# Three additions moved from GpSimd to VectorE, and parts of the retention branch issued one chunk earlier, in a two-layer decoder trunk

## The chip, the core and the metric

The kernel runs on one NeuronCore of a Trainium2 chip. A core has five instruction streams that run side by side and meet only at semaphores: TensorE (PE in the profile; its weight loads are listed as PEld), VectorE (DVE), ScalarE (ACT), GpSimd (POOL) and SyncE (SP), which here only issues weight transfers. The metric is the device time of one execution in microseconds (us), the median of several executions; lower is better.

## The reference

Two layers work on 256 tokens of width 2048 in float32. Each layer is a token mixer and a gated FFN, each behind an RMSNorm and added to the residual stream. The mixer has four branches (retention, a diagonal state-space model called S5, gated linear attention or GLA, and causal pooling). One input projection feeds them all, and it also makes one sigmoid gate per branch and channel:

```python
proj = (h @ w_in).astype(jnp.float32)
rq, rk, rv, rg, su, gq, gk, gv, gg, gr, pu, gate_logits = jnp.split(proj, _split_points(), axis=-1)
rq = rotary(rq.reshape(B_, S_, RET_HEADS, RET_DK), positions)
rk = rotary(rk.reshape(B_, S_, RET_HEADS, RET_DK), positions) * (RET_DK ** -0.5)
ra = retention(rq, rk, rv.reshape(B_, S_, RET_HEADS, RET_DV))
ya = head_norm(ra).reshape(B_, S_, BRANCH_W) * jax.nn.silu(rg)
...
branches = jnp.stack([ya, yb, yc, yd], axis=2)
up = jnp.einsum('bsnc,ncd->bsnd', branches, w_branch)
gates = jax.nn.sigmoid(gate_logits.reshape(B_, S_, N_BRANCH, D_MODEL))
merged = jnp.sum(gates * up, axis=2)
return merged @ w_out
```

Rotary is `x1*cos - x2*sin, x1*sin + x2*cos` for each head, so it ends in one addition of two products. Retention multiplies the scores of queries and keys by a causal decay and then by the values; `head_norm` normalises each of its four heads. `merged` is a sum over four branches, so three additions for each block of channels.

## The kernel before

**The weight stream.** All large products run through chunks. A chunk is 128 x 1024 weights (512 KB): SP brings it into one of three `raw` buffers, ScalarE casts it to `hi` (L262), VectorE subtracts to get `lo <- raw, hi` (L263), and TensorE multiplies first by `hi` and then by `lo`. `hi` and `lo` have three buffers each. In the mixer most chunks go through `mm_xs` (matmuls at L362, eight with `hi` and four with `lo`), where the activations `X` are the weights and the streamed side is `hi` or `lo`. Every chunk thus needs one cast of ScalarE and one subtraction of VectorE in time.

**The side work.** Branches are written as Python generators. After the instructions of each chunk have been emitted, `pump()` lets every started generator that is due go on to its next `yield`; `yield n` means that the next part comes n chunks later. TensorE's instructions stay in the order in which they are written, so the numbers behind `yield` set the place of each branch's matmuls between the chunks. The other engines are ordered by a scheduler with priorities: what stands under `with prio():` is put ahead of side work, as far as its inputs allow; the rest comes later.

**The places that matter here.** `retention` turns queries and keys (tile `rqk`, and `rot`, a copy with halves swapped) by two products on VectorE (L492, L493) and one addition on GpSimd (L494); then come the scores of two pairs of heads (L505), their product with the decay (tiles `P1`, `P2`, L508 and L509), the product with the values (L514 to L516), and `head_out`. `head_out` normalises on VectorE into `hy`, transposes `hy` on TensorE in two pairs of heads (L470) and splits each transposed pair into `br[:, :, 0]` and `br[:, :, 1]` (ScalarE's cast at L262 and VectorE's subtraction at L263, tile `br`). GLA uses the same `head_out`. Its first matmuls are L525 (tiles `grT`, `wg`) and L549 (tile `gqk`). All of these take their PSUM from `psmall()`, two buffers in turn, so a matmul of the side work waits until the buffer two requests back has been read. `up` adds a branch into the merged sum `mg` (L878): on GpSimd, except for the very last block. S5 uses GpSimd for four additions and subtractions in each of its steps (L747, L748, L758, L759), between products on VectorE.

Of the kernel before, what the change touches and what calls it, by code (L numbers as in the profile page):

```python
# [15 lines left out]
ALU = mybir.AluOpType  # L16
# [136 lines left out]
def trunk(ctx: ExitStack, tc, d, outT, dbg=None):  # L153
# [54 lines left out]
    def C(name):  # L208
        o, w = CON[name]
        return con[:, o:o + w]  # L210
# [10 lines left out]
    tt = nc.vector.tensor_tensor  # L221
# [3 lines left out]
    ptt = nc.gpsimd.tensor_tensor  # L225
# [4 lines left out]
    def order(then):  # L230

        tc.add_manual_dep(then.ins, anchor[0].ins.name, NOSYNC, reason="order")
        return then

    def prio(offset=4000):
        return tc.high_priority(offset=offset)
# [21 lines left out]
    def psmall():  # L258
        return P.small()

    def split(hi, lo, src):
        i = nc.scalar.copy(hi, src)  # L262
        tt(lo, src, hi.bitcast(F32), op=ALU.subtract)  # L263
        return i
# [82 lines left out]
    def mm_xs(kt, rows, X):  # L347

        ps = P.main.tile([128, 2, 512], F32, tag="mp", name="mp")
        for c in range(0, kt, 2):  # L350
            hi, lo, n = load(2, rows(c * 128, (c + 2) * 128))
            xs_chunk(ps, kt, c, hi, lo, X, (0, 1))
            pump()
        return ps
# [80 lines left out]
    def bc(ap, n):  # L435

        return ap.unsqueeze(1).to_broadcast([128, n, T])
# [4 lines left out]
    def head_out(pool, ops, sg, r, br, wait):  # L442

        st = pool.tile([128, 8, 6], F32, tag="hst", name="hst", bufs=1)
        mv = pool.tile([128, 8, 2], F32, tag="hmv", name="hmv", bufs=1)
        for t in range(2):
            for i in range(4):
                nc.vector.bn_stats(st[:, 4 * t + i, :], ops[t][:, i * 128:(i + 1) * 128])
        for i in range(8):
            nc.vector.bn_aggr(mv[:, i, :], st[:, i, :])  # L450
        ve = pool.tile([128, 8], F32, tag="hve", name="hve", bufs=1)
        ts(ve, mv[:, :, 1], EPS, None, op0=ALU.add)
        rs = pool.tile([128, 8], F32, tag="hrs", name="hrs", bufs=1)
        ptt(rs, ve, C("mhalf")[:, 0:8], op=ALU.pow)
        y = pool.tile([128, 2, 512], F32, tag="k4", name="hy", bufs=6)
        for t in range(2):
            ts(rs[:, 4 * t:4 * t + 4], rs[:, 4 * t:4 * t + 4], r[:, t:t + 1], 0.5,
               op0=ALU.mult, op1=ALU.mult)
            for i in range(4):
                ts(y[:, t, i * 128:(i + 1) * 128], ops[t][:, i * 128:(i + 1) * 128],  # L460
                   mv[:, 4 * t + i, 0:1], rs[:, 4 * t + i:4 * t + i + 1],
                   op0=ALU.subtract, op1=ALU.mult)
        tt(y, y, sg, op=ALU.mult)
        yield wait
        for i in range(4):
            if i % 2 == 0:
                ps = psmall()
            for t in range(2):
                o = (i % 2) * T + t * 128
                nc.tensor.transpose(ps[:, o:o + 128], y[:, t, i * 128:(i + 1) * 128], ident)  # L470
            if i % 2 == 1:
                s = ps[:, :].rearrange("p (a t) -> p a t", a=2)
                split(br[:, i - 1:i + 1, 0], br[:, i - 1:i + 1, 1], s)
                yield 2

    def silu_gate(pool, ps, rh):

        sg = pool.tile([128, 2, 512], F32, tag="k4", name="sg", bufs=6)
        with prio():
            for t in range(2):  # L480
                act(sg[:, t], ps[:, t], AF.Tanh, scale=rh[:, t:t + 1])
                stt(sg[:, t], sg[:, t], 1.0, ps[:, t], op0=ALU.add, op1=ALU.mult)
        return sg

    def retention(pool, qk, rv, sg, r, br):
        rot = pool.tile([128, 4, T], F32, tag="k4", name="rot", bufs=6)

        for b in (0, 32, 64, 96):
            o = b ^ 32
            order(nc.scalar.dma_start(rot[b:b + 32], qk[o:o + 32]))  # L490
        yield 3
        tt(rot, rot, bc(sinr, 4), op=ALU.mult)  # L492
        tt(qk, qk, bc(cosr, 4), op=ALU.mult)  # L493
        ptt(rot, rot, qk, op=ALU.add)  # L494
        yield 8
        dec = pool.tile([128, 4, T], F32, tag="k4", name="dec", bufs=6)
        order(nc.scalar.dma_start(dec, d["decay"].rearrange("p (h t) -> p h t", h=4)))
        P1 = pool.tile([128, 4, T], F32, tag="k4", name="P1", bufs=6)
        P2 = pool.tile([128, 4, 128], F32, tag="k2", name="P2", bufs=4)
        for a in range(2):  # L500
            pss = [psmall(), psmall()]
            for o, sc, t0 in ((0, slice(0, 128), 0), (T, slice(128, T), 128)):
                for j, ps in enumerate(pss):
                    b = slice(64 * j, 64 * j + 64)
                    nc.tensor.matmul(ps[:, o:o + T - t0], rot[b, 2 + a, sc], rot[b, a, t0:T],  # L505
                                     start=(o == 0), stop=True, **MM)
            for j, ps in enumerate(pss):
                tt(P1[:, 2 * a + j], ps[:, 0:T], dec[:, 2 * a + j, :], op=ALU.mult)  # L508
                tt(P2[:, 2 * a + j], ps[:, T:384], dec[:, 2 * a + j, 0:128], op=ALU.mult)  # L509
            yield 2  # L510
        ops = [psmall(), psmall()]
        for hd in range(4):
            e = slice(hd * 128, (hd + 1) * 128)
            nc.tensor.matmul(ops[0][:, e], P1[:, hd, 0:128], rv[:, 0, e], start=True, stop=True, **MM)  # L514
            nc.tensor.matmul(ops[1][:, e], P1[:, hd, 128:T], rv[:, 0, e], start=True, stop=False, **MM)
            nc.tensor.matmul(ops[1][:, e], P2[:, hd], rv[:, 1, e], start=False, stop=True, **MM)  # L516
        yield from head_out(pool, ops, sg, r, br, 12)

    def gla(pool, l, V, qk, grT, gv, sg, r, br):
        wg = pool.tile([32, 256], F32, tag="k1", name="wg", bufs=1)  # L520
# [80 lines left out]
        for hd in range(4):  # L601
# [6 lines left out]
            nc.tensor.matmul(ops[1][:, e], A[:, j, a0 + 128:a0 + 256], gv[:, 1, e],  # L608
                             start=False, stop=True, **MM)
        yield from head_out(pool, ops, sg, r, br, 8)  # L610

    def pooling(pool, l, V, ps, rb, br):
# [204 lines left out]
    def wcols(w, c0, n):  # L817
        return lambda r0, r1: [w[r0:r1, c0:c0 + n]]
# [22 lines left out]
    def mixer(l, V, X, R, outer, pool):  # L841
# [20 lines left out]
        def gate(n, blk):  # L862

            ps = projx(C_GATE + n * D + blk * 512)
            th = outer.tile([128, 2, 512], F32, tag="th", name="th", bufs=1)
            with prio():
                for t in range(2):
                    act(th[:, t], ps[:, t], AF.Tanh, scale=rh[:, t:t + 1])
            return th

        def up(n, blk, br, th, m, first=False):
            ps = mm_xs(4, wcols(d["w_branch"][l, n], blk * 512, 512), br)
            with prio():
                if first:
                    stt(m, th, 1.0, ps, op0=ALU.add, op1=ALU.mult)
                else:
                    stt(th, th, 1.0, ps, op0=ALU.add, op1=ALU.mult)  # L877
                    (tt if n == 1 and blk == 3 else ptt)(m, m, th, op=ALU.add)  # L878


        ps = proj(C_PU)
        r, rb = R.r, R.rb
# [26 lines left out]
        sg = silu_gate(pool, ps, rh)  # L909
        br_ret = branch_tiles(outer)  # L910
        start(retention(pool, rqk, rv, sg, r, br_ret))

        gqk = pool.tile([128, 4, T], F32, tag="k4", name="gqk", bufs=6)
# [12 lines left out]
        sg = silu_gate(pool, ps, rh)  # L926
# [13 lines left out]
        for n, br in ((3, br_pool), (0, br_ret), (2, br_gla)):  # L940
            for blk in range(4):
                th = gate(n, blk)
                up(n, blk, br, th, mg[:, :, blk * 512:(blk + 1) * 512], first=(n == 3))
# [7 lines left out]
        split_scaled(br_s5[:, :, 0], br_s5[:, :, 1], y5, 0.25)  # L951
        ths = [gate(1, 0)]
        return mg, gate, up, br_s5, ths

    def turn(mg, blk, M):
# [13 lines left out]
    for l in range(DEPTH):  # L969
        last = l + 1 == DEPTH  # L970
        with tc.tile_pool(name=f"mix{l}", bufs=1, reuse_waits="tile") as outer, ExitStack() as mixb:
            with narrow(l):
                with tc.tile_pool(name=f"mixa{l}", bufs=1, reuse_waits="tile") as pool:
                    mg, gate, up, br_s5, ths = mixer(l, V, X, R, outer, pool)
                pool = mixb.enter_context(tc.tile_pool(name=f"mixb{l}", bufs=1, reuse_waits="tile"))
# [36 lines left out]
        with tc.tile_pool(name=f"ffn{l}", bufs=1, reuse_waits="tile") as pool, extra_raw(l):  # L1012
            G = pool.tile([128, KF, 2, T], F32R, tag="g", name="G")
            wup = d["w_up"][l]
            for b0 in range(0, KF, 2):
# [6 lines left out]
                with prio():  # L1022
                    u = pool.tile([128, 4, T], F32, tag="u", name="u")
                    uc = pool.tile([128, 4, T], F32, tag="uc", name="uc")
                    n = 2 * nt
                    for i, ps in enumerate(pss):
                        m = slice(2 * i, 2 * i + 2)
# [18 lines left out]
            for k, n in ((0, 4), (4, 4), (8, 4), (12, 3), (15, 1)) if last else ((0, 4), (4, 4), (8, 4), (12, 4)):  # L1046
                m = slice(k, k + n)
# [37 lines left out]
```

## Time and profile before

| what | value |
|---|---|
| time, median of 3 runs | 2987.28 us (2987.2 to 2988.97) |
| the profiled execution's own time | 2986.73 us |
| its span, first to last instruction | 2984.9 us |
| TensorE busy | 2950.4 us (99%) |
| VectorE busy | 2104.4 us (71%) |
| ScalarE busy | 1524.7 us (51%) |
| GpSimd busy | 381.8 us (13%) |
| mean granted TensorE clock | 0.996 of full speed |

The first mixer runs from the start to about 690 us, its FFN to about 1480 us; the second layer repeats this to the end. In a row of a timeline the first number is the start and the second the duration; `xN` counts merged instructions, and square brackets hold the idle time of the engine just before the row and who ended it. TensorE's matmuls overlap in the profile (each is shown longer than its turn), so progress is read from start to start.

### The profile page before, as it was taken

The page shows a single profiled execution, that of the slowest core. Times are in us where ns is not written, and L with a number is a line of the kernel's source. Part 1 is how long each engine was busy: PE and PEld are TensorE (multiplying, and loading weights), DVE is VectorE, ACT ScalarE, POOL GpSimd, SP SyncE. Part 2 cuts the span into 40 slices and gives each one's busy share as a digit, 9 for nine tenths or more (in the row PEclk, how much of TensorE's full clock was granted, in tenths as well). Part 3 has the DMA queues.
Part 4 walks back from the last instruction along what each step waited for, and adds up shares of the span by engine and source line. Part 5 has one row for each costly group of instructions (what it writes and reads, how often), then busy time and mean ns, then how long its engine had stood idle before and what let it go on. Part 6 is the DMA issues. An engine that isn't in the chain of part 4 may idle for free.

```text
span 2984.9 us, 42650 instructions
## 1 busy us (share of the span) xinstructions
PE 2950.4 (99%) x15952; PEld 2525.5 (85%) x15952; DVE 2104.4 (71%) x2712; ACT 1524.7 (51%) x1906; POOL 381.8 (13%) x371
## 2 busy tenths in 40 slices
PE   8999999999999999999999999999999999999998
PEld 8877887888888888888898788878888888888887
DVE  7798888556677777755568888885567777776445
ACT  5545545444555555544444555554445555555443
POOL 6311122010000000000053111221010000000001
PEclk9999999999999999999999999999999999999999
DMA  7765666666566666666576566666666666666554
GB/s 228 200 181 163 188 178 186 206 189 212 187 188 191 191 187 195 193 196 195 181 209 196 164 179 179 185 186 205 188 212 186 193 186 192 190 187 193 187 180 148
DMA packets 416176, 565.87 MB, mean 190 GB/s; under 512 B 24736, under 2 KB 258656, under 8 KB 415968
## 3 DMA queue, kind: packets, MB, share of 16 engines
q1 hardware_dynamic: 404960, 545.58, 59.7%
q10 hardware_dynamic: 11008, 17.57, 1.9%
q8 instruction: 125, 2.05, 0.3%
q14 instruction: 83, 0.68, 0.1%
HBM read 554.66 MB, written 4.19 MB: 187 GB/s over the span
## 4 chain that ended last, share of the span: by engine, by line
PE 91%; DVE 4%; issue 1%; DMA 1%; ACT 1%; POOL 0%; SPq 0%; DVEq 0%; ACTq 0%; POOLq 0%
PE mp L339 38%; PE mp L362 30%; PE mp L342 20%; DVE lo L263 2%; PE mp L320 2%; DMA raw<-w_in 1%; PE ps L578 1%; ACT hi L262 1%; DVE s L757 0%; PE pbu L767 0%; PE ps L961 0%; DVE s_cos L737 0%; PE pbu L796 0%; DMA h<-xT 0%; DMA raw<-w_branch 0%
## 5 line engine op out<-in xcount | busy, mean ns | idle before, releaser
L263 DVE TENSOR_TENSOR lo<-raw,hi 128x1024 fp32r<-128x1024 f32 (+2 forms) x1043 | 1319.0, 1267 | 752.9 <-ACT hi L262 748.6
L262 ACT CAST hi<-raw 128x1024 fp32r<-128x1024 f32 (+2 forms) x1043 | 1084.9, 1041 | 1199.9 <-PE mp L339 682.9
L339 PE MATMUL mp<-X,hi 128*128 128x512 f32 x3136 | 1088.7, 394 | 0.0
L342 PE MATMUL mp<-X,lo 128*128 128x256 f32 x3136 | 869.8, 277 | 0.6 <-DVE lo L263 0.6
L339 PEld LDWEIGHTS mp<-X,hi 128*128 128x128 f32 x3136 | 588.0, 187 | 135.8
L362 PE MATMUL mp<-hi,X 128*128 128x512 f32 x2560 | 641.9, 393 | 0.0
L342 PEld LDWEIGHTS mp<-X,lo 128*128 128x128 f32 x3136 | 589.3, 188 | 1.0 <-DVE lo L263 0.9
L362 PEld LDWEIGHTS mp<-hi,X 128*128 128x128 f32 x2560 | 478.1, 189 | 103.2 <-issue 1.4
L339 PE MATMUL mp<-G,hi 128*128 128x512 f32 x1376 | 477.2, 390 | 0.0
L342 PE MATMUL mp<-G,lo 128*128 128x256 f32 x1376 | 388.1, 282 | 0.0
L362 PE MATMUL mp<-lo,X 128*128 128x512 f32 x1280 | 344.5, 391 | 5.0 <-DVE lo L263 5.0
L339 PEld LDWEIGHTS mp<-G,hi 128*128 128x128 f32 x1376 | 258.3, 188 | 54.1
L362 PEld LDWEIGHTS mp<-lo,X 128*128 128x128 f32 x1280 | 240.3, 188 | 59.1 <-DVE lo L263 9.3
L342 PEld LDWEIGHTS mp<-G,lo 128*128 128x128 f32 x1376 | 260.2, 189 | 0.1
L381 POOL TENSOR_TENSOR ss<-ss,sq 128x256 f32<-128x256 f32 x55 | 56.9, 1034 | 1464.2 <-ACT sq L380 1454.9
L339 PE MATMUL mp<-M,hi 128*128 128x512 f32 x512 | 177.9, 391 | 0.0
L342 PE MATMUL mp<-M,lo 128*128 128x256 f32 x512 | 144.4, 282 | 0.0
L362 PE MATMUL mp<-hi,br 128*128 128x512 f32 x512 | 130.2, 396 | 0.2 <-ACT hi L262 0.2
L362 PEld LDWEIGHTS mp<-hi,br 128*128 128x128 f32 x512 | 95.5, 188 | 23.8 <-issue 0.8
L878 POOL TENSOR_TENSOR mg<-mg,th 128x1024 f32<-128x1024 f32 x22 | 69.7, 3170 | 352.2 <-DVE th L877 342.9
L339 PEld LDWEIGHTS mp<-M,hi 128*128 128x128 f32 x512 | 96.1, 188 | 20.1
L1033 ACT ACTIVATE uc<-u,vec 128x256 f32<-128x256 f32 x172 | 89.6, 591 | 15.0 <-DVE u L1030 15.0
(228 smaller groups left out, 2134.0 us busy)
## 6 DMA issues: line engine op xcount, KB each, us to landing
raw<-w_in SPq DMA_DIRECT2D x383, 512.0 KB, 3.8
raw<-w_up SPq DMA_DIRECT2D x688, 256.0 KB, 3.3
raw<-w_down SPq DMA_DIRECT2D x152, 512.0 KB, 4.3
raw<-w_branch SPq DMA_DIRECT2D x64, 512.0 KB, 4.3
raw<-w_out SPq DMA_DIRECT2D x64, 512.0 KB, 4.4
raw<-w_down SPq DMA_DIRECT2D x21, 384.0 KB, 3.8
rB<-sB ACTq DMA_DIRECT2D x8, 384.0 KB, 4.9
U<-us ACTq DMA_DIRECT2D x96, 32.0 KB, 3.4
```

Source lines behind the costliest of these rows:

```text
L262: i = nc.scalar.copy(hi, src)
L263: tt(lo, src, hi.bitcast(F32), op=ALU.subtract)
L320: nc.tensor.matmul(ps[:, j, :], a[:, k, sl], X[:, kk, b, :], start=(kk == 0 and i == 0 and j % 2 == 0), stop=(kk == kt - 1 and i == 2), **MM)
L339: nc.tensor.matmul(ps.rearrange("p a t -> p (a t)"), hi[:, k, sl], X[:, kk].rearrange("p a t -> p (a t)"), start=(kk == 0), stop=(kk == kt ...
L342: nc.tensor.matmul(ps[:, 0], lo[:, k, sl], X[:, kk, 0, :], start=False, stop=(kk == kt - 1), **MM)
L362: nc.tensor.matmul(ps[:, j, :], X[:, c + k, a, j * 128:(j + 1) * 128], w[:, k, :], start=(c + k == 0 and a == 0 and w is hi), stop=(c + k ...
L381: (tt if k >= 12 else ptt)(ss, ss, sq, op=ALU.add)
L578: nc.tensor.matmul(ps[:, i * 128:(i + 1) * 128], x, x, start=True, stop=True, **MM)
L878: (tt if n == 1 and blk == 3 else ptt)(m, m, th, op=ALU.add)
L1033: act(uc[:, j], u[:, j], AF.Identity, bias=V("cb", ci), scale=V("cw2", ci))
```

## The change

Four edits. The addition that ends the rotation (L494 before, L495 after) and the additions of the merged sum (L878 before, L879 after) are issued on VectorE; all of the latter were on GpSimd but the last block's. Scores, and with them what follows in the retention generator, come one chunk earlier (`yield 8` to 7), and the transposes of `hy` one more (wait 12 to 11). In `head_out` the second pair of heads follows the first after one chunk, not two (`yield 2` to 1), for GLA too, and the split of a transposed pair gets priority. One line is added, so line numbers behind L472 are higher by one after the change.

```diff
@@ head_out
             if i % 2 == 1:
                 s = ps[:, :].rearrange("p (a t) -> p a t", a=2)
-                split(br[:, i - 1:i + 1, 0], br[:, i - 1:i + 1, 1], s)
-                yield 2
+                with prio():
+                    split(br[:, i - 1:i + 1, 0], br[:, i - 1:i + 1, 1], s)
+                yield 1
@@ retention
         tt(rot, rot, bc(sinr, 4), op=ALU.mult)
         tt(qk, qk, bc(cosr, 4), op=ALU.mult)
-        ptt(rot, rot, qk, op=ALU.add)
-        yield 8
+        tt(rot, rot, qk, op=ALU.add)
+        yield 7
...
-        yield from head_out(pool, ops, sg, r, br, 12)
+        yield from head_out(pool, ops, sg, r, br, 11)
@@ up
                     stt(th, th, 1.0, ps, op0=ALU.add, op1=ALU.mult)
-                    (tt if n == 1 and blk == 3 else ptt)(m, m, th, op=ALU.add)
+                    tt(m, m, th, op=ALU.add)
```

TensorE, from GLA's matmul L525 to its matmul L549, in the order of before (`grT`, `wg`: GLA's gate; `con`, `hy`: the transposes of the retention output; `gqk`: GLA's queries and keys):

```order
L525 MATMUL ps<-grT,wg 128x256 x2
L362 MATMUL mp<-hi,X 128x512 x8
L362 MATMUL mp<-lo,X 128x512 x4
L362 MATMUL mp<-hi,X 128x512 x8
L362 MATMUL mp<-lo,X 128x512 x4
L470 MATMUL ps<-con,hy 128x128 x4
L362 MATMUL mp<-hi,X 128x512 x8
L362 MATMUL mp<-lo,X 128x512 x4
L362 MATMUL mp<-hi,X 128x512 x8
L362 MATMUL mp<-lo,X 128x512 x4
L470 MATMUL ps<-con,hy 128x128 x4
L549 MATMUL ps<-gqk 128x128 x8
```

The same stretch of TensorE's order after the change, where L525 is L526 and L549 is L550:

```order
L470 MATMUL ps<-con,hy 128x128 x4
L526 MATMUL ps<-grT,wg 128x256 x2
L362 MATMUL mp<-hi,X 128x512 x8
L362 MATMUL mp<-lo,X 128x512 x4
L470 MATMUL ps<-con,hy 128x128 x4
L362 MATMUL mp<-hi,X 128x512 x8
L362 MATMUL mp<-lo,X 128x512 x4
L362 MATMUL mp<-hi,X 128x512 x8
L362 MATMUL mp<-lo,X 128x512 x4
L362 MATMUL mp<-hi,X 128x512 x8
L362 MATMUL mp<-lo,X 128x512 x4
L550 MATMUL ps<-gqk 128x128 x8
```

Before, the second transposes stood directly in front of L549. After, three chunks lie between them, and one chunk and L526 lie between the first and the second transposes.

VectorE around the rotation, in the order of before:

```order
L493 TENSOR_TENSOR rqk<-rqk,cosr 128x1024
L263 TENSOR_TENSOR gr_1530<-wgr,gr_1530 128x16x16
L263 TENSOR_TENSOR lo<-raw,hi 128x1024
L853 TENSOR_TENSOR gqk<-gqk,mp 128x512
L263 TENSOR_TENSOR lo<-raw,hi 128x1024
L860 TENSOR_TENSOR gqk<-gqk,rb 128x512
```

The same place of VectorE after the change:

```order
L494 TENSOR_TENSOR rqk<-rqk,cosr 128x1024
L263 TENSOR_TENSOR gr_1530<-wgr,gr_1530 128x16x16
L263 TENSOR_TENSOR lo<-raw,hi 128x1024
L854 TENSOR_TENSOR gqk<-gqk,mp 128x512
L495 TENSOR_TENSOR rot<-rot,rqk 128x1024
L861 TENSOR_TENSOR gqk<-gqk,rb 128x512
L263 TENSOR_TENSOR lo<-raw,hi 128x1024
```

The addition L495 and the scaling L861 now stand ahead of the second `lo`. The additions of the merged sum stand in VectorE's order behind one `lo` that follows the gating product L878.

## Rows read from the trace of the kernel before

**Rows 1.** The page, busy time, share of the span, instructions:
```profile
PE 2950.4 (99%) x15952; PEld 2525.5 (85%) x15952; DVE 2104.4 (71%) x2712; ACT 1524.7 (51%) x1906; POOL 381.8 (13%) x371
```
**Rows 2.** TensorE's waits: us in total, times, longest us:
```profile
PE ps L549 <- DVE br L263: 6.1, 2, 3.9
PE mp L362 <- DVE lo L263: 5.0, 10, 1.3
```
**Rows 3.** Timeline, TensorE at L549, first layer, then second layer:
```profile
220.80 1.98 PE L362 MATMUL mp<-hi,X 128*128 128x512 f32 x8
222.62 1.07 PE L362 MATMUL mp<-lo,X 128*128 128x512 f32 x4
...
226.76 1.16 PE L549 MATMUL ps<-gqk 64*128 64x128 f32 x14 [2.22 <-DVE br L263]
227.85 3.28 PE L362 MATMUL mp<-hi,X 128*128 128x512 f32 x8
230.92 1.53 PE L362 MATMUL mp<-lo,X 128*128 128x512 f32 x4
...
1704.03 2.07 PE L549 MATMUL ps<-gqk 64*128 64x128 f32 x14 [3.93 <-DVE br L263]
1706.03 3.78 PE L362 MATMUL mp<-hi,X 128*128 128x512 f32 x8
```
**Rows 4.** Windows: busy PE, PEld, DVE, ACT, POOL; granted clock; DMA:
```profile
1700.00:1710.00 10.00, 6.07 (x25) 4.93 (x25) 7.46 (x17) 5.34 (x11) 0.00 (x0) 0.66 0.35 105
```
**Rows 5.** Timeline, the split behind the second transposes, second layer:
```profile
1702.14 0.56 ACT L262 CAST br<-ps 128x512 fp32r<-128x512 f32 x1
...
1703.30 0.68 DVE L263 TENSOR_TENSOR br<-ps,br 128x512 fp32r<-128x512 f32 x1
```
**Rows 6.** Timeline around the rotation's addition, first layer:
```profile
155.09 2.57 POOL L494 TENSOR_TENSOR rot<-rot,rqk 128x1024 f32<-128x1024 f32 x1
...
155.34 3.41 DVE L263 TENSOR_TENSOR lo<-raw,hi 128x1024 fp32r<-128x1024 f32 x1
...
158.80 1.20 PE L362 MATMUL mp<-lo,X 128*128 128x512 f32 x4 [1.33 <-DVE lo L263]
...
159.27 1.21 DVE L263 TENSOR_TENSOR lo<-raw,hi 128x1024 fp32r<-128x1024 f32 x1
```
**Rows 7.** Timeline around a merged-sum addition, first layer, near 490 us:
```profile
485.94 3.24 POOL L878 TENSOR_TENSOR mg<-mg,th 128x1024 f32<-128x1024 f32 x1 [0.36 <-DVE th L877]
...
486.86 2.48 DVE L737 TENSOR_SCALAR s_cos<-s_cos 128x256 f32<-128x256 f32 x1
...
491.12 1.21 PE L362 MATMUL mp<-lo,X 128*128 128x512 f32 x4 [0.70 <-DVE lo L263]
...
498.24 0.97 PE L362 MATMUL mp<-lo,X 128*128 128x512 f32 x3 [0.55 <-DVE lo L263]
```
**Rows 8.** Timeline, another merged-sum addition, near 362 us:
```profile
359.41 0.28 DVE L737 TENSOR_SCALAR s_cos<-s_cos 128x256 f32<-128x256 f32 x1
...
362.24 3.26 POOL L878 TENSOR_TENSOR mg<-mg,th 128x1024 f32<-128x1024 f32 x1 [4.69 <-issue]
...
363.82 2.76 DVE L263 TENSOR_TENSOR lo<-raw,hi 128x1024 fp32r<-128x1024 f32 x1
```
**Rows 9.** Windows, columns as in rows 4, the end of the side work:
```profile
400.00:500.00 100.00, 98.29 (x463) 79.39 (x462) 90.50 (x147) 48.97 (x59) 25.57 (x23) 1.00 0.59 177
```
**Rows 10.** The merged sum's tile: the last block's addition on VectorE, ns:
```profile
L878 DVE TENSOR_TENSOR mg<-mg,th x2: 1218/1218/1219, 686.8 to 2164.8; 128x1024 f32<-128x1024 f32 x2
```
**Rows 11.** Timeline, L525, first transposes and their split, first layer:
```profile
210.98 1.12 PE L525 MATMUL ps<-grT,wg 32*128 32x256 f32 x4
...
217.62 0.60 PE L470 MATMUL ps<-con,hy 128*128 128x128 f32 x4
...
220.16 0.57 ACT L262 CAST br<-ps 128x512 fp32r<-128x512 f32 x1
...
220.89 0.68 DVE L263 TENSOR_TENSOR br<-ps,br 128x512 fp32r<-128x512 f32 x1
```

## The prediction

> **What bounds the kernel now.** I read the page first: TensorE is busy 2950.4 us of a span of 2984.9 us [rows 1], so no engine's busy time can be shortened to good effect unless TensorE waits for it, and no edit takes a matmul away. The question is what TensorE waits for, and the list of its waits answers it. Apart from the start and the end of the program two kinds are left: L549 waits twice for the subtraction that fills `br`, 6.1 us together, and matmuls with `lo` wait ten times for VectorE's L263, 5.0 us together [rows 2]. Then I read the timeline at each of them. At L549 the wait is 2.22 us in the first layer and 3.93 us in the second [rows 3]; the reader is to see there that the matmuls behind it are slow as well, and in the table of windows that the granted clock is 0.66 between 1700 and 1710 us [rows 4]: behind an idle TensorE the clock stands at the lower of its two levels, 1.2 instead of 2.4 GHz, for a while. The `lo` waits lie where VectorE has most to do: one at the rotation [rows 6], three in a row near 490 us, the first and the last of which are shown [rows 7], and their counterparts in the second layer. From 400 to 500 us VectorE is busy 90.50 of 100 us [rows 9].
>
> **The wait at L549 (term 1).** It is there because the second transposes stand directly in front of L549 and L549 needs their buffer back, which is free only when both halves of the split are done. In the second layer the cast starts at 1702.14 and the subtraction ends at 1703.98 [rows 5], late because other casts and subtractions were put ahead. Its cost:
> - first layer: 2.22 idle; then eight `hi` matmuls in 3.28 instead of 1.98, and four `lo` ones in 1.53 instead of 1.07 [rows 3]: 2.22 + 1.30 + 0.46 = 3.98 us;
> - second layer: 3.93 idle; then L549's fourteen in 2.07 instead of 1.16, and eight `hi` matmuls in 3.78 instead of 1.98 [rows 3]: 3.93 + 0.91 + 1.80 = 6.64 us.
>
> Together 10.6 us. After the change three chunks stand between the second transposes and this matmul. A chunk takes TensorE 2.73 us (twelve matmuls; 222.62 - 220.80 for eight) [rows 3], so the split has 8.2 us, against the 3.95 us that the first split took (below). I count the whole 10.6 us as gone; what keeps L549 waiting next would be the conversion of L525's result, which is issued a chunk earlier than the second split.
>
> **What is late next (term 2, a loss).** The second transposes now need the buffer of the first ones, with only L525 and one chunk between: 0.35 + 1.06 + 2.73 = 4.1 us from the first transposes to the second (L525 takes about its 1.12) [rows 3, 11]. Before, the first split ended 221.57 - 217.62 = 3.95 us after the first transposes [rows 11]. With the same delays the wait would be nothing. The priority brings ScalarE's cast forward, but VectorE's half still stands behind two `lo` subtractions (1.21 each), the copy into `grT` and a few S5 products; counting these from the moment `grT` can be written, VectorE ends it about 1 us late. Bounds: 0, and a wait as long as 3.93 with the slow matmuls behind it. I take 1.0 us for each layer, without the slow clock, since the 1.33 us wait of rows 6 is followed by `lo` matmuls of 1.20 in all, near the usual 1.07: a loss of 2.0 us. Behind the waiting transposes stand the chunks of the stream; they resume at once, because `hi` and `lo` get filled meanwhile.
>
> **Rotation's addition on VectorE and scores a chunk earlier (term 3).** The addition takes GpSimd 2.57 us, and the `lo` subtraction issued beside it takes 3.41 instead of 1.21 [rows 6]: VectorE stood still for 2.2 us, and TensorE 1.33. On VectorE an addition of this shape takes 1.22 (the last block's is one already) [rows 10], so VectorE has 1.0 us more here, and the `lo` that was late is 2.2 us earlier. But TensorE then reaches the scores sooner, and the scores stand a chunk earlier too. They need the addition. On VectorE it ends near 158.4 us: 155.34 + 1.21 for the `lo`, some 0.6 for an addition of half the size, and 1.22. Without its wait TensorE is there at the same time: 158.80 - 1.33 + 0.91 for four matmuls [rows 3, 6]. The products with the decay, the products with values and GLA's L525 follow, each with less time in front than before. So I let half of the 1.33 come back, 0.6 us. In the second layer this wait is small already, and I count nothing. Ends: the whole 1.33 gained; or 1.5 us lost in each layer, a wait of the same length at a score or at the values.
>
> **Merged-sum additions on VectorE (term 4).** Eleven a layer leave GpSimd. On GpSimd one takes 3.24 us, and the VectorE instruction beside it is held: L737 takes 2.48 instead of 0.28, a `lo` 2.76 instead of 1.21 [rows 6 to 8], so 2.20 and 1.55 us are lost on VectorE against 1.22 for the addition itself [rows 10]. That is a gain of 1.0 us at 486 us and of 0.3 at 362. Five of a layer's eleven lie before the last of the three waits; the others come when the side work is over, where no wait for `lo` is in the list, and are worth nothing either way. TensorE waits 0.70 first and 0.55 last of three near 490 us, some 1.7 us a layer. VectorE is what is late there, so each us that it saves comes off: 1.0 us a layer, 2.0 in all. Ends: 1.7 a layer; or a loss of 5 x 1.22 = 6.1 a layer if holding is not saved (the second rival).
>
> A rule of the Trainium skill stands against these two terms: Perfetto Trace Analysis, "Optimizing Scalar/DVE Operations", says that work may well be given to GpSimd where VectorE is saturated, and adds that the two share an SBUF read port, so it may not help. SBUF — State Buffer, "Who interferes with whom", sharpens the second half: whichever starts first holds the port for its whole instruction. The held rows agree with the second half; by the first alone the sum would end on the slow side, as in the second rival.
>
> **The rest.** GLA's second transposes come a chunk earlier as well; nothing waits behind them in the list of waits, and I count 0 (ends: 0.5 either way). The load of the decay table moves on ScalarE's queue with the scores, ahead of one cast: one issue, and I count 0 (end: a cast later by less than one `lo`, 1.2 us, in each layer). SP's order of weight loads is unchanged.
>
> **Sum.** -10.6 + 2.0 - 0.6 - 2.0 = -11.2 us. Against the profiled execution's own 2986.73 us that gives 2975.5; the median of the runs is 0.55 higher, so I forecast 2976 us.
>
> **The rivals.**
> - *All of it comes back.* Neither the second transposes nor the scores wait, and the ten `lo` waits go: -10.6 - 5.0 = -15.6, so 2971.5 us. For it: priority on the split, and 8.2 us of room. Against: VectorE is 90% busy and gets 1.22 us for every addition. 17 in 100.
> - *VectorE becomes the bound, slower than before.* Its place is 360 to 500 us of each mixer. If the held time of rows 7 and 8 is only time that VectorE would have waited anyhow for ScalarE's cast or for a transfer, nothing is saved: six additions a layer (five and the rotation's) cost 1.22 each on the path, 14.6 us in all, against the 10.6 of term 1: +4.0, so 2991 us. It decides once less than about 0.9 us of each hold is saved (12 additions, 10.6 us). For it: three waits for `lo` in a row near 490. Against: L737 needs only data that ScalarE had long made, and its 2.48 us end with GpSimd's addition. 4 in 100.
> - *The wait only moves.* The second transposes wait as long as L549 did, with the slow clock behind; terms 3 and 4 alone remain: -2.6, so 2984.5 us. For it: two buffers in turn, one chunk of room, and a 3.95 us split against 4.1. Against: the cast has priority now. 10 in 100. That the edits do not do what they say can be left out: the order shows them.
>
> **How the numbers follow.** My forecast has the other 69 in 100; its own range is 2973 to 2980, from term 2 between 0 and 4 and term 3 at its ends. The range of 8 in 10 reaches into the first rival and most of the way to the third: 2970 to 2983. A measurement of this kernel tells 0.2%, 6 us, from no change: below 2981.3 is faster. Forecast and first rival lie there but for about 2 in 100: 84. Within: 12, the third rival and those 2. Slower: 4.
>
> **What would show it.** In the profile after, TensorE's wait at L550 (once L549) for `br` is gone, and the clock stays at 1.00 there. A wait of about 1 us stands at the second transposes. The `lo` beside the rotation takes 1.2 us, L738 0.3 us, and the three waits near 490 us are below 1 us together. I am wrong if TensorE's granted clock falls in the same place, if L470 waits more than 2 us, or if waits for `lo` add up to more than 5 us.

## The result and the profile after

The changed kernel takes 2966.93 us, median of 4 runs (2965.81 to 2969.09), against 2987.24 us (2986.61 to 2988.97) for the kernel before: a ratio of 0.9935, 95% interval 0.9923 to 0.9947, or 20.3 us less. The forecast was 2976, its range 2970 to 2983. The direction was right; the gain came out nearly twice as large, and 3 us beyond the low end. The profiled execution took 2965.81 us, span 2964.0, mean granted clock 0.998.

Busy time first. The row answers to [rows 1]:

```profile
PE 2938.8 (99%) x15952; PEld 2521.9 (85%) x15952; DVE 2091.4 (71%) x2736; ACT 1525.8 (51%) x1906; POOL 324.7 (11%) x347
```

VectorE has 24 instructions more, each of 1.22 us, and is nevertheless busy 13 us less: it is held less often, and that saves more than it took over. Then TensorE's waits, the whole list, to be set against [rows 2]:

```profile
PE mp L320 <- ACT hi L262: 6.4, 2, 5.7
PE mp L320 <- DVE lo L263: 2.4, 3, 1.1
PE ps L395 <- DVE ss L381: 2.0, 1, 2.0
PE ps L607 <- DVE gA L599: 1.6, 2, 0.9
PE ps L408 <- DVE dg L404: 1.5, 1, 1.5
PE mp L342 <- DVE lo L263: 0.3, 1, 0.3
```

L550 (L549 before) and all ten `lo` waits at L362 are gone; L607 is new. The other five belong to the start, the norms, the FFN and the end, where nothing was changed.

**The place of term 1.** TensorE at L550 in the first layer, against [rows 3]; then the windows around it in both layers, against [rows 4], with the same columns:

```profile
219.81 1.16 PE L550 MATMUL ps<-gqk 64*128 64x128 f32 x16
220.91 2.11 PE L362 MATMUL mp<-hi,X 128*128 128x512 f32 x8
```
```profile
219.00:229.00 10.00, 10.00 (x55) 8.03 (x55) 8.88 (x18) 8.33 (x14) 0.00 (x0) 1.00 0.54 154
1690.00:1700.00 10.00, 10.00 (x46) 8.23 (x46) 9.29 (x19) 7.17 (x12) 0.73 (x2) 1.00 0.58 164
```

All sixteen matmuls run in one piece, the `hi` ones behind them take their usual 2.1 us, and the granted clock is 1.00, the 2.4 GHz level, where it was 0.66 on the mean.

**The place of term 2.** TensorE from the first to the second transposes, then the VectorE instructions that matter in this stretch, against [rows 11]:

```profile
206.66 0.60 PE L470 MATMUL ps<-con,hy 128*128 128x128 f32 x4
207.18 1.13 PE L526 MATMUL ps<-grT,wg 32*128 32x256 f32 x4
208.24 2.12 PE L362 MATMUL mp<-hi,X 128*128 128x512 f32 x8
210.19 1.07 PE L362 MATMUL mp<-lo,X 128*128 128x512 f32 x4
211.10 0.60 PE L470 MATMUL ps<-con,hy 128*128 128x128 f32 x4
```
```profile
204.90 0.40 DVE L935 TENSOR_TENSOR grT<-ps,rb 32x256 f32<-32x256 f32 x1
...
209.44 0.68 DVE L263 TENSOR_TENSOR br<-ps,br 128x512 fp32r<-128x512 f32 x1
```

No bracket stands at the second transposes: they come 4.44 us behind the first ones, and the split is done after 3.46 (209.44 + 0.68 - 206.66).

**The place of term 3.** VectorE at the rotation, against [rows 6], then TensorE with both pairs of scores:

```profile
153.53 1.21 DVE L263 TENSOR_TENSOR lo<-raw,hi 128x1024 fp32r<-128x1024 f32 x1
...
155.27 1.21 DVE L495 TENSOR_TENSOR rot<-rot,rqk 128x1024 f32<-128x1024 f32 x1
```
```profile
156.81 0.92 PE L506 MATMUL ps<-rot 64*128 64x256 f32 x8
...
163.35 0.92 PE L506 MATMUL ps<-rot 64*128 64x256 f32 x8
```

The `lo` beside the addition takes 1.21 us, not 3.41, and the addition ends at 156.48, 0.3 us ahead of the scores. Before, the second scores looked like this, in the weight loads and then in the matmuls:

```profile
169.35 0.29 PEld L505 LDWEIGHTS ps<-rot 64*128 64x128 f32 x2 [0.52 <-DVE P L509]
169.35 1.45 PE L505 MATMUL ps<-rot 64*128 64x256 f32 x8
169.88 0.73 PEld L505 LDWEIGHTS ps<-rot 64*128 64x128 f32 x6 [0.23 <-DVE P L509]
```

Eight matmuls of the same shape were drawn over 1.45 us instead of 0.92, because they waited for the decay products before and inside the group. The list of TensorE's waits [rows 2] does not show this wait, and I had not seen it.

**The place of term 4.** VectorE near 478 us, against [rows 7], where L737 took 2.48:

```profile
477.51 1.21 DVE L879 TENSOR_TENSOR mg<-mg,th 128x1024 f32<-128x1024 f32 x1
478.65 1.21 DVE L263 TENSOR_TENSOR lo<-raw,hi 128x1024 fp32r<-128x1024 f32 x1
479.79 0.28 DVE L738 TENSOR_SCALAR s_cos<-s_cos 128x256 f32<-128x256 f32 x1
```

The window of [rows 9], where VectorE was busy 90.50 of 100 us:

```profile
400.00:500.00 100.00, 99.12 (x470) 81.15 (x469) 84.33 (x141) 53.28 (x63) 18.82 (x17) 1.00 0.62 186
```

The three waits near 490 are gone. Before, the held L737 of [rows 7] and one product more stood ahead of the next `lo`:

```profile
489.38 0.42 DVE L743 TENSOR_TENSOR s<-pbu,s_cos 128x256 f32<-128x256 f32 x1
489.83 1.23 DVE L263 TENSOR_TENSOR lo<-raw,hi 128x1024 fp32r<-128x1024 f32 x1
```

Now this `lo` stands directly behind the addition, and L738 and the product after it come later. Ahead of it VectorE spends 1.21 us instead of 2.48 + 0.42: 1.0 of that is the forecast saving (2.20 held, less 1.22), the other 0.7 is the new order, which the forecast did not have.

**The new wait** stands at GLA's product with the values. VectorE first, then TensorE:

```profile
414.47 1.22 DVE L879 TENSOR_TENSOR mg<-mg,th 128x1024 f32<-128x1024 f32 x1
415.61 0.42 DVE L599 COPY gA<-ps 128x256 f32<-128x256 f32 x1
415.94 1.22 DVE L263 TENSOR_TENSOR lo<-raw,hi 128x1024 fp32r<-128x1024 f32 x1
417.08 0.42 DVE L599 COPY gA<-ps 128x256 f32<-128x256 f32 x1
```
```profile
417.64 0.46 PE L607 MATMUL ps<-gv,gA 128*128 128x128 f32 x2 [0.88 <-DVE gA L599]
```

The merged sum's addition now stands in VectorE's own order ahead of the copies into `gA`, so the second copy, behind one more `lo`, is late.

**Where the 20.9 us of the two profiled executions lie.** TensorE has 15,136 matmuls into `mp`, in the same order in every kernel here. Taking the start of the n-th in one trace from that of the n-th in the trace before gives the time gained or lost up to there, and the difference of two such numbers that of a stage. Both layers together, in us (minus is gained); stages between those named are within 0.2 us, and the two FFNs within 0.02 (0.11 with the `head_out` edit alone). The column of the rotation ends ahead of L525, so it also holds a small `lo` wait at 200.71 us and one at 1676.26 us (0.17 and 0.19 listed):

| kernel | start | rotation to second scores | L525 to L549 and behind | GLA's values | near 490 and 1970 | all |
|---|---|---|---|---|---|---|
| the changed kernel | -1.5 | -4.5 | -11.4 | +1.9 | -5.45 | -21.0 |
| merged sum alone on VectorE | -0.6 | -0.1 | +0.1 | +2.1 | -5.45 | -4.0 |
| rotation alone on VectorE | -1.0 | -3.1 | -0.1 | -0.3 | -0.3 | -4.8 |
| `head_out` edit alone | +0.2 | -0.2 | -8.1 | +0.5 | +1.5 | -6.0 |
| scores and transposes moved alone | -0.3 | -0.2 | -11.4 | -0.3 | -0.1 | -12.3 |
| changed, both additions back on GpSimd | -0.3 | -0.2 | -11.4 | +0.2 | +1.6 | -10.1 |
| changed, without the `head_out` edit | -1.3 | -4.4 | -11.4 | +2.3 | -5.45 | -20.3 |
| changed, without priority for the split | -0.1 | -4.1 | -11.4 | +2.4 | -5.45 | -18.6 |
| changed, idle GpSimd additions added | -0.5 | -4.5 | -11.4 | +10.4 | -5.2 | -11.2 |
| changed, priority for the copies into `gA` | -0.4 | -4.2 | -11.4 | -0.3 | -5.45 | -21.7 |
| the same without the `head_out` edit | +0.2 | -4.5 | -11.4 | -0.3 | -5.45 | -21.4 |

The start, 150 us in which no kernel differs from another, varies from +0.2 to -1.5 between executions. The 1.5 that the changed kernel's profile shows there is chance, not a gain. The cost of a slow clock varies too: with the rotation alone the place of L549 is 1.3 us slower in the first layer and 1.4 faster in the second, at waits of nearly the same length (2.06 and 3.67 us), and the -0.1 in the table is their sum.

### The profile page after: what moved, and what is told of

It reads as the page before. It is cut to its first block, busy times and chain, and to the rows that moved or that the text cites. A ratio compares the mean times of both kernels' runs of the same rounds, so it can differ in the third digit from the quotient of the medians.

```text
span 2964.0 us, 42589 instructions
## 1 busy us (share of the span) xinstructions
PE 2938.8 (99%) x15952; PEld 2521.9 (85%) x15952; DVE 2091.4 (71%) x2736; ACT 1525.8 (51%) x1906; POOL 324.7 (11%) x347
## 4 chain that ended last, share of the span: by engine, by line
PE 98%; DVE 1%; ACT 0%; DMA 0%; issue 0%; POOL 0%; SPq 0%; DVEq 0%; ACTq 0%; POOLq 0%
PE mp L339 39%; PE mp L362 35%; PE mp L342 20%; PE mp L320 2%; PE ps L579 1%; DVE lo L263 0%; PE pbu L768 0%; PE pbu L797 0%; PE ps L962 0%; ACT hi L262 0%; DMA h<-xT 0%; DVE hg L1065 0%; DVE X L268 0%; PE ps L470 0%; PE ps L932 0%
## 5 line engine op out<-in xcount | busy, mean ns | idle before, releaser
L263 DVE TENSOR_TENSOR lo<-raw,hi 128x1024 fp32r<-128x1024 f32 (+2 forms) x1043 | 1286.7, 1235 | 743.5 <-ACT hi L262 740.3
L362 PE MATMUL mp<-hi,X 128*128 128x512 f32 x2560 | 639.1, 392 | 0.0
L362 PEld LDWEIGHTS mp<-hi,X 128*128 128x128 f32 x2560 | 476.5, 188 | 101.9 <-issue 1.2
L362 PE MATMUL mp<-lo,X 128*128 128x512 f32 x1280 | 342.7, 390 | 0.0
L362 PEld LDWEIGHTS mp<-lo,X 128*128 128x128 f32 x1280 | 240.4, 188 | 50.0
L362 PE MATMUL mp<-hi,br 128*128 128x512 f32 x512 | 130.2, 396 | 0.0
L362 PEld LDWEIGHTS mp<-hi,br 128*128 128x128 f32 x512 | 95.7, 188 | 23.2 <-issue 0.8
L342 PEld LDWEIGHTS mp<-M,lo 128*128 128x128 f32 x512 | 97.0, 190 | 0.1
```

The source lines that it names most:

```text
L342: nc.tensor.matmul(ps[:, 0], lo[:, k, sl], X[:, kk, 0, :], start=False, stop=(kk == kt - 1), **MM)
L362: nc.tensor.matmul(ps[:, j, :], X[:, c + k, a, j * 128:(j + 1) * 128], w[:, k, :], start=(c + k == 0 and a == 0 and w is hi), stop=(c + k ...
```

## The experiments

My theory was that each term stands for itself: moves end the wait at L549, VectorE's additions end the held instructions, nothing else matters. The rivals were that `head_out`'s edit (priority, one chunk instead of two) is what makes the gain; that the additions gain nothing by themselves; and that the gain of VectorE's additions has nothing to do with holding.

**Merged sum alone.** The kernel before with

```diff
-                    (tt if n == 1 and blk == 3 else ptt)(m, m, th, op=ALU.add)
+                    tt(m, m, th, op=ALU.add)
```

> The kernel before with one edit: all additions of the merged sum on VectorE. Theory A (a GpSimd addition holds the VectorE instruction beside it; 1.2 us on VectorE are cheaper than 1.5 to 2.2 us held): the three waits for lo near 490 us and near 1970 us go, TensorE gains 2.7 to 3.2 us at each, and GLA's product with the values (L605 to L608) waits 0.9 to 1.3 us in each layer because an addition now stands ahead of the copies L598; the wait at L549 stays. About -3.6 us, so 2983.6. Rival B (the waits near 490 went because the side work before them had moved up): the waits near 490 stay at 0.4 us or more each, and the time is 2987 or above.

Measured: 2982.68 against 2985.9, ratio 0.9987 (0.9978 to 0.9997), 3.2 us less. Its waits:

```profile
PE ps L549 <- DVE br L263: 6.0, 2, 3.9
...
PE ps L606 <- DVE gA L598: 1.9, 2, 1.1
PE mp L362 <- DVE lo L263: 1.8, 4, 1.2
```

The `lo` waits fall from ten to four; those left are at the rotation and at 201 us, and their counterparts in the second layer; the wait for `gA` comes with this edit and with no other.

**Rotation alone.** The kernel before with

```diff
-        ptt(rot, rot, qk, op=ALU.add)
+        tt(rot, rot, qk, op=ALU.add)
```

> The kernel before with one edit: the rotation's addition on VectorE. Theory A: the lo beside it takes 1.2 us instead of 3.4, its wait (1.33 us idle, 1.5 from start to start, in the first layer; 0.4 in the second) goes, and as the scores stay where they were nothing new waits: -1.9 to -2.5 us, so 2985. Rival B (that wait went because the scores were moved): it stays, and the time is within 1 us of before.

Measured: 2983.8 against 2985.9, ratio 0.9992 (0.9983 to 1.0002): by the times alone it can't be told from no change. The trace decides where the times can't. The wait of 1.33 us at the rotation is gone, the `lo` there takes 1.21, and the stage is 3.1 us shorter, both layers together. L549 stays:

```profile
PE ps L549 <- DVE br L263: 5.7, 2, 3.7
PE mp L362 <- DVE lo L263: 3.3, 6, 0.9
```

**`head_out` alone.** The kernel before with

```diff
-                split(br[:, i - 1:i + 1, 0], br[:, i - 1:i + 1, 1], s)
-                yield 2
+                with prio():
+                    split(br[:, i - 1:i + 1, 0], br[:, i - 1:i + 1, 1], s)
+                yield 1
```

> The kernel before with the edit of head_out alone: priority for the split, and one chunk instead of two between the transposes. One chunk (2.73 us) then stands between the second transposes and GLA's L549 (now L550). Theory A (the wait there is the latency of the split, and the slow matmuls behind follow a long wait): the split with priority ends some 3 to 3.5 us after the transposes, so 0.3 to 1 us of wait is left and no slow clock: -9.5 to -11 us, so about 2977. Rival C (priority is not what shortens the split; VectorE's queue is): 2 us of wait are left in each layer and the clock falls again in one of them, -4 to -6 us.

Measured: 2980.61 against 2985.9, ratio 0.9983 (0.9973 to 0.9992). The place gives 8.1 us, less than expected, since the wait is shortened and not ended. The matmul in both layers, then the window of the second:

```profile
225.24 1.16 PE L550 MATMUL ps<-gqk 64*128 64x128 f32 x14 [0.67 <-DVE br L263]
...
1699.34 1.16 PE L550 MATMUL ps<-gqk 64*128 64x128 f32 x14 [1.54 <-DVE br L263]
```
```profile
1698.00:1706.00 8.00, 6.66 (x38) 5.58 (x39) 7.30 (x15) 6.36 (x11) 0.00 (x0) 1.00 0.46 132
```

What goes first is the clock's share: behind a wait of 1.54 us the granted clock stays at 1.00 and the fourteen matmuls take 1.16 us, where behind 3.93 us they took 2.07 [rows 3]. The total, 5.3 us less, lies in the range that was given for rival C, but not for its reason: the waits are shorter than 2 us and the clock does not fall. What was not expected is a loss behind L550, 0.5 us at GLA's values and 1.5 near 490 and 1970 (table). It appears again below, where `head_out`'s edit stands with the additions on GpSimd, and not where they are on VectorE; no run shows its cause.

**The moves alone.** The kernel before with

```diff
-        yield 8
+        yield 7
...
-        yield from head_out(pool, ops, sg, r, br, 12)
+        yield from head_out(pool, ops, sg, r, br, 11)
```

> The kernel before with the two moved yields alone (scores one chunk earlier, transposes one more); no priority, and two chunks between the transposes as before. Two chunks (5.5 us) then stand between the second transposes and L549. Theory A (chunks in front of L549 are what counts): split without priority takes 4 to 4.9 us, the wait is gone, and so is the slow clock: -11 to -12 us at this place. At the scores TensorE still waits for the addition on GpSimd, now a chunk nearer: 1 to 2 us more there in the first layer. In all -9 to -11, so about 2977. Rival C (priority is what counts): a wait of 1 us or more stays at L549.

Measured: 2975.96 against 2985.9, ratio 0.9965 (0.9952 to 0.9978). Two numbers changed by one make about half of the gain: L549 is gone from the list without `head_out`'s edit, since two more chunks now stand between the second transposes and it. Most waits for `lo` stay, and the second scores, a chunk earlier, now show theirs in the list:

```profile
PE mp L362 <- DVE lo L263: 4.7, 8, 1.2
...
PE ps L505 <- DVE P L509: 1.0, 2, 0.5
```

That costs 0.4 us in each layer, less than the 1 to 2 expected, and the small `lo` waits at 201 and 1676 us, which are gone here, give back 0.5 each.

**The changed kernel without `head_out`'s edit.** That edit undone, the rest kept.

```diff
-                with prio():
-                    split(br[:, i - 1:i + 1, 0], br[:, i - 1:i + 1, 1], s)
-                yield 1
+                split(br[:, i - 1:i + 1, 0], br[:, i - 1:i + 1, 1], s)
+                yield 2
```

> The changed kernel with the edit of head_out undone (no priority, two chunks between the transposes): three of the four edits. Theory A (with the moved yields alone, two chunks stood in front of L549 and its wait was gone, 12.3 us at the end of the two stages): L549 does not wait here either, and the time is within 1.5 us of the changed kernel's, about 2967. Rival C (VectorE, which now has the additions too, needs the priority): a wait of 0.5 us or more at L549 or at the second transposes, 2 us or more in all.

Measured: 2966.9 against 2987.02, ratio 0.9932 (0.9917 to 0.9946): the changed kernel's time. The rival that this edit makes the gain falls.

**Without the priority alone.** The split is issued as before, `yield 1` stays.

```diff
-                with prio():
-                    split(br[:, i - 1:i + 1, 0], br[:, i - 1:i + 1, 1], s)
+                split(br[:, i - 1:i + 1, 0], br[:, i - 1:i + 1, 1], s)
```

> The changed kernel without the priority of the split, its one chunk between the transposes kept. Forecast's term (the second transposes wait for the first split, 4.1 us of room against 4 us): a wait of 0.5 to 1.5 us at L470 in each layer, 1 to 3 us in all. Rival: the split has time anyway; no wait at L470, within 0.5 us of the changed kernel in the profile.

Measured: 2966.94, ratio 0.9932 (0.9917 to 0.9947). TensorE's transposes, then the split's second half:

```profile
208.51 0.60 PE L470 MATMUL ps<-con,hy 128*128 128x128 f32 x4
...
212.95 0.60 PE L470 MATMUL ps<-con,hy 128*128 128x128 f32 x4
```
```profile
211.43 0.68 DVE L263 TENSOR_TENSOR br<-ps,br 128x512 fp32r<-128x512 f32 x1
```

The split ends 3.60 us behind the first transposes (211.43 + 0.68 - 208.51); the second come after 4.44. The priority is not what keeps the second transposes from waiting.

**Both additions back on GpSimd.** The changed kernel with `ptt` at L495 and at L879.

```diff
-        tt(rot, rot, qk, op=ALU.add)
+        ptt(rot, rot, qk, op=ALU.add)
...
-                    tt(m, m, th, op=ALU.add)
+                    (tt if n == 1 and blk == 3 else ptt)(m, m, th, op=ALU.add)
```

> The changed kernel with both kinds of additions back on GpSimd: the moved yields and the edit of head_out alone. What is asked is why the second transposes did not wait. If it was because VectorE had been relieved (the rotation's addition), it is behind here and the wait that was forecast appears: 0.5 to 1.5 us at L470 in each layer; TensorE also waits at the rotation (1.4 us, first layer) and near 490 us. If the room was simply under-counted (4.4 us from transposes to transposes against 3.5 to 3.6 for the split), no wait at L470 appears either, and the stage of L550 gains as in the changed kernel, 5.1 and 7.5 us. In all -11 to -13 us, 2974.5.

Measured: 2976.51 against 2986.03, ratio 0.9969 (0.9957 to 0.998). VectorE's additions are thus worth 9.6 us on top of the rest (2976.51 - 2966.93), where terms 3 and 4 had 2.6. The size depends on the rest: without `head_out`'s edit the traces, freed of their starts, put the same additions at 7.0 us (-19.0 against -12.0), since the loss that `head_out` brings with GpSimd's additions is not there. The waits that come back:

```profile
PE mp L362 <- DVE lo L263: 5.6, 8, 1.2
...
PE ps L506 <- DVE P L510: 1.0, 2, 0.5
```

The second transposes do not wait here either: the split ends 2.6 us behind the first ones. So it is not the relief of VectorE that keeps term 2 at nothing.

**Is it the holding?** Here GpSimd is given work of its own again: beside each merged sum's addition but the last it adds a tile to itself four times, 128x256 each, and the result is never used.

```diff
                     stt(th, th, 1.0, ps, op0=ALU.add, op1=ALU.mult)
+                    if not (n == 1 and blk == 3):
+                        junk = sm.tile([128, T], F32, tag="sq", name="sq")
+                        for i in range(4):
+                            s = slice(256 * (i % 2), 256 * (i % 2) + 256)
+                            ptt(junk, th[:, i // 2, s], th[:, i // 2, s], op=ALU.add)
                     tt(m, m, th, op=ALU.add)
```

> The changed kernel with an idle GpSimd addition of the same size put beside each of VectorE's merged-sum additions (four of 128x256, tile th to a spare tile, read by nobody; output unchanged). Theory A (GpSimd holds VectorE): lo subtractions beside them take 2 to 3 us instead of 1.2, waits for lo near 490 and 1970 us come back with 2.5 to 5 us in each layer, so +5 to +10 us over the changed kernel. Rival B (what counted was who waits for the sum, not the port): VectorE's durations stay at 1.2 us and the time within 1 us.

Measured: 2975.64, ratio 0.9962 (0.9948 to 0.9976), 8.7 us above the changed kernel. GpSimd, then VectorE beside it, then the waits:

```profile
354.71 5.27 POOL L883 TENSOR_TENSOR sq<-th 128x256 f32<-128x256 f32 x4 [4.69 <-DVE th L878]
```
```profile
355.62 1.64 DVE L884 TENSOR_TENSOR mg<-mg,th 128x1024 f32<-128x1024 f32 x1
357.19 1.63 DVE L263 TENSOR_TENSOR lo<-raw,hi 128x1024 fp32r<-128x1024 f32 x1
```
```profile
PE mp L362 <- DVE lo L263: 2.5, 2, 1.3
PE ps L606 <- DVE gA L599: 2.4, 2, 1.4
...
PE ps L607 <- DVE gA L599: 2.3, 2, 1.2
```

The addition and the `lo` beside it take 0.42 us longer each than in the changed kernel, with the same data. These two rows wait for nothing of GpSimd's, and are longer only for its work beside them. The Trainium skill says of such a pair (SBUF — State Buffer, "Who interferes with whom") that a VectorE instruction with two SBUF inputs contends with a GpSimd instruction that reads SBUF. This run agrees: 1.64 and 1.63 us instead of 1.22 and 1.21.

Holding is not all of the 8.7 us, though. From 386 to 403 us VectorE falls 1.4 us behind the changed kernel; 0.8 of it are two rows like these, and most of the rest is an S5 instruction (L751) that waits 0.30 us for a GpSimd subtraction queued behind the idle additions and is itself 0.5 us longer. TensorE then waits 1.26 us for `lo` at 400.58 us and, in the first layer, 1.07 and 1.15 us at GLA's values, behind which the granted clock is 0.72 from 420 to 426 us and eight pairs of matmuls take 3.4 instead of 1.9 us. The place I had wrong: the time is lost at 400 to 426 us and in the same stage of the second layer, not near 490, where no wait comes back. So the run shows that GpSimd's work lengthens VectorE's instructions beside it, and that TensorE pays for it; how much of the 5.45 us near 490 and 1970 is holding, and how much the new order, no run separates.

**The new wait taken away.** The changed kernel with the copies into `gA` under priority.

```diff
-                    nc.vector.tensor_copy(A2[:, j, :], ps[:, 0:T])
+                    with prio():
+                        nc.vector.tensor_copy(A2[:, j, :], ps[:, 0:T])
```

> The changed kernel with priority for GLA's two copies into A2 (L599), which puts them ahead of the merged-sum addition in VectorE's order. Theory A (the wait at L607, 1.33 and 0.99 us late in the two layers, is the addition standing ahead of the copies): both waits go, -2.0 to -2.3 us in the profile, about 2964.7. Rival: the copies wait for TensorE's scores, and the wait stays.

Measured: 2964.88, median of 4 (2964.54 to 2965.06), against 2987.02; ratio 0.9924 (0.991 to 0.9939). VectorE:

```profile
415.14 0.75 DVE L600 COPY gA<-ps 128x256 f32<-128x256 f32 x2
415.81 1.21 DVE L880 TENSOR_TENSOR mg<-mg,th 128x1024 f32<-128x1024 f32 x1
```

Both copies now stand ahead of the addition, L607 waits no more, and the stage goes from +1.9 to -0.3 us. The median is 2 us below the changed kernel's, from another set of runs, and the two intervals against the kernel before overlap. In its own set two variants that run in the changed kernel's time (without `head_out`'s edit, without the priority alone) took 2966.45 us or more in all eight executions, and this one 2965.06 or less in all four. Together with the stage that shows the gain. The same with `head_out`'s edit undone as well:

> The changed kernel with the priority for GLA's copies and with the edit of head_out undone: the shortest set of edits that should keep every gain. Theory A: same as the run with the copies' priority alone, within 1 us, 2964.9.

Measured: 2965.07 (2964.71 to 2965.89), ratio 0.9932 (0.9915 to 0.9948). It gives the same, without `head_out`'s edit.

## Why the prediction was right in direction and too small

The sum was -11.2 us; the traces show -21.0, of which 1.5 is the start's chance. By its steps:

- **Term 1, the wait at L549: right.** Forecast -10.6, measured -11.4 in every kernel that has the moves. The clock's share was rightly counted from the slow matmuls. The cause of the gain is the two moves; `head_out`'s edit alone gets 8.1, and on top of the moves nothing at this place.
- **Term 2, the second transposes: wrong.** The step that failed reads "counting these from the moment `grT` can be written, VectorE ends it about 1 us late". In the trace `grT` is written at 204.90, before the first transposes, and behind the transposes VectorE has one whole `lo` and three short S5 instructions to do ahead of the split, not two `lo` and the copy into `grT`: 3.46 us instead of some 5. The room was 4.44, not 4.1, because L526 starts 0.52 us behind the transposes and the chunk takes 2.86. The 3.95 us of [rows 11], which I had before me and set aside, would have said no wait. The runs without priority and with GpSimd's additions show the same, at 3.60 and 2.6 us. So +2.0 became 0.
- **Term 3, rotation and scores: the step "So I let half of the 1.33 come back" was wrong, and so was the nothing for the second layer.** Forecast -0.6, measured -4.5. The addition's end, forecast near 158.4, came at 156.48; 1.49 of that difference is the start's chance, so the addition itself was placed to 0.4 us. It ends 0.33 us ahead of the scores, nothing behind it waits, and none of the 1.33 came back. Of the 2.8 us in the first layer about 1.6 are the wait of [rows 6] with what the list leaves out (below) and the longer matmuls behind it, 0.7 the wait at the second scores, and 0.5 the `lo` wait at 200.71 us. The second scores started 1.16 us behind the `lo` group, where 1.00 is usual (163.35 - 162.35 after), and lost 0.53 inside; in the first layer this wait goes only when the addition and the moves come together. In the second layer the same 0.7 and two small `lo` waits make 1.7.
- **Term 4, the merged sum: the step "each us that it saves comes off: 1.0 us a layer" was too small, and a new wait was unforeseen.** Forecast -2.0. Near 490 and 1970 the traces show -5.45, more than the end of 1.7 a layer: all three waits went, with what the list leaves out (below). VectorE saved the 1.0, and its `lo` also moved ahead of other work (the place of term 4). The new wait at L607 gave back 1.9 (2.1 with this edit alone). Net -3.6. I had asked what waits for `lo`, and not what stands behind the addition in VectorE's order.

Ahead of the new wait terms 3 and 4 gained 9.95 us (4.5 + 5.45) where 2.6 was forecast. Of the 7.35 missing, 2.4 is listed idle time that I did not count as gone (5.0 in [rows 2], 2.6 taken). The next 3.0 comes from taking listed idle time as the price of a wait. A matmul of a chunk is drawn 392 ns long, but its turn is 227 ns (1.82 us for eight), so the first 165 ns of each wait are hidden under the drawn end of the matmul before, and the four `lo` matmuls behind a wait take 1.21 instead of 1.07: 0.3 us a wait, for ten waits. The two waits at the second scores, which I had not seen, are 1.4. These add up to 6.8; the remaining 0.5 I can't place.

**The rivals.** The nearest was that all comes back, 2971.5 us: neither transposes nor scores wait and the `lo` waits go. That is what happened, but for L607; its price was too small for the reason just given. VectorE did not become the bound: it is busy 84.33 instead of 90.50 us from 400 to 500. Against this rival stood the held L737, and the run with idle GpSimd work bears that out. The wait did not move.

The rule that I had weighed against the change is one of the Trainium skill (Perfetto Trace Analysis, "Optimizing Scalar/DVE Operations"): work may be given to GpSimd where VectorE is saturated. The same section adds that the two share an SBUF read port, so that it might not help. Here it did not help: with both kinds of additions back on GpSimd the kernel is 9.6 us slower, and 7 us of that lie near 490 and 1970 us, where VectorE was 90% busy before.

In the traces the parts add up: merged sum, rotation and moves, each alone and without the start, gave -3.4, -3.8 and -12.0, together -19.2; the changed kernel without its start has -19.5. That holds for the traces, one execution of each; the medians of the runs give 3.2 + 2.1 + 9.9 = 15.3 us for the three against 20.3, each known to about 3 or 4 us either way, so they neither confirm nor refute it. GLA's second transposes and the decay table, counted at nothing, made no wait in the changed kernel.

## What to carry to other kernels

Where two engines contend, price an instruction on the one by what its neighbour on the other loses, and not by busy shares: an addition that took GpSimd 3.2 us cost VectorE 1.55 to 2.2 us, and on VectorE itself 1.22. Price a wait of TensorE by starts, not by the idle time listed, and look for groups drawn longer than the same group elsewhere. When an instruction is moved to a busy in-order engine, name what is queued behind it there: here that was a copy for which TensorE then waited, and putting the copy ahead gave back the loss.

## What the runs showed of the hardware

- **A shorter wait kept the clock.** Behind idle stretches of TensorE of 2.22 and 3.93 us the matmuls were slow [rows 3]; behind 0.67 and 1.54 us, at the same place, the granted clock stayed at 1.00. Shortening a wait can thus gain more than its idle time. It is not safe to count on: in the run with idle GpSimd additions two waits of 1.07 and 1.15 us close together were followed by slow matmuls (granted 0.72 from 420 to 426 us), while 1.38 and 1.16 us at the same place of the second layer were not (1.00).
- **Short GpSimd instructions hold less each, but delay both.** One GpSimd addition of 3.2 us held its VectorE neighbour for 1.55 to 2.2 us [rows 7, 8]. Four short ones held two VectorE instructions by 0.42 us each, and took 5.27 us themselves, where GpSimd's S5 additions of the same 128x256 shape take 0.74 us each when undisturbed.
- **The start differs from execution to execution** by up to 1.7 us with nothing changed in it, which is more than one edit here is worth. It has to be taken out before two traces are compared.
